# Splits on VectorE, gates one token group at a time, and candidate sums on GpSimd, in a two-block transformer kernel

## The chip, the cores and the metric

The kernel runs on one core of one Trainium2 chip. The core has five engines that run side by side, each with its own instruction queue in fixed order: TensorE (PE, matrix products; PEld is its weight load), VectorE (DVE), ScalarE (ACT), GpSimd (POOL) and SyncE (SP, which issues the transfers). The metric is the device time of one execution in microseconds (us), lower being better. The kernel before takes 1712.33 us, the median of three runs from 1710.88 to 1713.65.

## The reference

There are 256 tokens of 1024 features in fp32, and two blocks. The first adds to the tokens an attention and a recurrent mixer, and then a layer of experts that are looked up by keys; the part that the change touches is this layer:

```python
def peer_ffn(xn, wq, subkeys, u_tab, v_tab):
    q = (xt @ wq).reshape(T, PEER_HEADS, 2, PEER_HALF)
    s = jnp.einsum('thpd,hpnd->thpn', q, subkeys)
    top_s, top_i = lax.top_k(s, PEER_TOPK)
    cand_s = (top_s[:, :, 0, :, None] + top_s[:, :, 1, None, :]).reshape(...)
    best_s, best_j = lax.top_k(cand_s, PEER_TOPK)
    idx = jnp.take_along_axis(cand_i, best_j, axis=-1)
    gates = jax.nn.softmax(best_s, axis=-1)
    ...
    hdn = gelu(einsum('cd,chkd->chk', xc, u_tab[idx])) * gates
    out = einsum('chk,chkd->cd', hdn, v_tab[idx])
```

It has 8 heads, 2 halves of 128 keys, 16 best of each half, 16 best of their sums, and so 16 of 16,384 experts per head and token. The second block is a retention layer (`_retention_layer`), a layer norm, an attention with compressed keys (`_mla_layer`), and a layer norm; each is made of products of the tokens with large weights:

```python
    x = _layer_norm(DEEPNORM_ALPHA * x + y, ln_g[layer], ln_b[layer])
```

## The kernel before

**Products and splits.** Every weight comes from HBM in pieces of 128 by 1024 (`raw`). A product is made of three matmuls on rounded halves (`mm3`, whose matmuls are at line 344): ScalarE copies a piece to a rounded `whi`, and the rest `wlo` = `raw` − `whi` is one subtraction of 128x1024 on VectorE or GpSimd. This is called a split here. `split_next` issues a split when one of four places (`room`) is free, and chooses the engine of the subtraction by a letter: pieces of `peer_u` have "U" (GpSimd as long as `ex["pool_free"]` is true, else VectorE), those of `peer_v` "V" (VectorE), many others "A":

```python
            v, g = flow.clock["V"], flow.clock["G"]
            eng = "G" if g < v + state["slack"] else "V"
```

**The order of the work.** The program is written by generators. A planner (`Flow`) keeps an estimated clock for every engine; the main blocks run in a row (`flow.run`), and at each of their `yield`s the chains started by `flow.spawn` are looked at: a chain goes on when the planner's TensorE clock has passed the time that it yielded (`SOON` is an offset to that time), or when the condition it yielded holds. So the order of instructions on each engine is fixed when the program is written, by the planner's clocks and by where `yield` stands. Every engine's instruction goes through one helper, at line 264, so the profile names instructions by tiles.

**The experts.** All 16,384 experts are computed densely, in 64 steps of 256, and the gates choose: `up(i)` multiplies the tokens with a step of `peer_u` (48 products of 256 columns per half, into a bank `sm` of the accumulator memory), `weigh(i)` multiplies by the gate matrix, and `down(i)` multiplies with `peer_v` (24 products of 512 columns per half step, into `mm`). 22 `up` steps run before the first `down`, since the gates come late.

**The search.** Per head, `top_keys(h)` multiplies queries by keys, copies the scores to `s_`, and `best16` takes the 16 best of each of four rows on VectorE (`v` values, `w` values with those found struck out, `i` places). Then four additions make the candidate sums `cd`, and a second `best16` takes the 16 best of them (`bs`, `bj`). `ex["best"]` orders the heads. After heads 3 and 7 `decode(g)` turns the places into keys for four heads: it is about 80 small VectorE instructions, sets `pool_free` to false, and its end transposes the indices and gates (`GI`) on TensorE into `GT`.

**The gates.** `dense_gates` builds the gate matrix `gd` in four parts of 32 key rows each, the first (n = 0) before the first `down`, the others during the `up`/`down` turns. `gate_steps` takes groups of 8 tokens: VectorE writes `oq`, `oe` and two `op` per group, TensorE makes 16 (n = 0) or 8 (n > 0) matmuls into one `sm` bank, ScalarE copies, and for n > 0 VectorE adds the two halves (`gd<-sm,glo`), which frees the bank. The table `GATES` holds, for n = 0 and n > 0, the number of chains and the number of groups per step. At this time there are four `mm` and four `sm` banks, which `up` and the gates share.

**The second block.** Its layers run as products on TensorE with short chains between them: norms and rotations on VectorE (`rn_`, `l_r`, `lat`, `klat_`, `qlat_`, `ql`), and small products on GpSimd (`qr`, `ro`, `klfl`, `qlfl`). Before it, `state["slack"] = SLACK2` is set (line 1927), with the letter "A" for most pieces.

Of the kernel before, what the change touches and what calls it, by code (L numbers as in the profile page):

```python
# [287 lines left out]
NB = 32  # L288
LEAD = 16
AHEAD = 6  # L290
SOON = -600.0
NT = 8
CUT = 384
ADA0 = 3
SLACK = 2500.0
SLACK2 = 2000.0
NRAW = 4
NF = 8
BANKS = (3, 5)
# [4 lines left out]
NSP2 = 8  # L304
NL = 2
HOLD2 = 7
GATES = ((3, 1), (2, 2))
NGP = 4
HOLD3 = 8

# [2 lines left out]
def tile_blocks(ctx: ExitStack, tc: tile.TileContext, a, out):  # L313
# [3 lines left out]
    flow = Flow()  # L317
    V, G, S = Engine(nc.vector, flow, "V"), Engine(nc.gpsimd, flow, "G"), Engine(nc.scalar, flow, "S")
# [16 lines left out]
    def mm(o, l, r, first=True, last=True):  # L335
        n, m = r.free_size(), l.free_size()
        if l.dtype == F32:
            ns = max(4 * n / 2.36, 2 * m / 1.2)
        elif l.dtype == F32R:
            ns = n / 2.3 + 7.0  # L340
        else:
            ns = max(29.0, n / 2.4 + 2.5)
        flow.op("P", ns, o, (l, r))
        P.matmul(o, l, r, start=first, stop=last)  # L344

    def bank(tag="sm"):
        return psum["tiles"].tile([128, 512], F32, name=tag, tag=tag, bufs=psum[tag])
# [13 lines left out]
    def cst(name):  # L361
        k, s, e = TABS[name]
        return tabs[k][:, s:e]
# [17 lines left out]

        return (None, fn, src, None)

    ex = {"rest": 0, "sums": 0, "top": 0, "best": 0, "gates": 0, "built": 0, "used": 0, "pool_free": True}
    state = {"whole": 0, "dma": 0, "split": 0, "at": 0, "inuse": 1, "inuse2": 0, "slack": SLACK}
    raws, parts, came, freed, ring, nostart, spare = {}, {}, {}, [], {}, set(), set()
    whole, whole_freed = {}, []
# [114 lines left out]
    def piece(name, ch):  # L502
        pass_over()
        i = state["at"]
        assert order[i][0] == name and order[i][1] == ch, (order[i][:2], name, ch)
        state["at"] += 1
        if order[i][3] == "F":
            return raws.pop(i), i
        return parts.pop(i)
# [8 lines left out]
    def soon():  # L518

        pass_over()  # L520
        if order[state["at"]][3] == "F":
            more()
            yield flow.written[raws[state["at"]].name]
            return
        while state["at"] not in parts:
            more()
            if state["at"] not in parts:
                yield flow.written[raws[state["at"]].name]
        yield came[state["at"]]

    def mm3(o, wh, wl, xh, xl, first, last):
        mm(o, wh, xh, first, False)
        mm(o, wh, xl, False, False)
        mm(o, wl, xh, False, last)
# [365 lines left out]
    rest = order[before + 128:]  # L900
# [524 lines left out]
    gates = []  # L1425
# [136 lines left out]
    def wqt_turn(blk, tt, q):  # L1562
        yield 0
        if tt == 0:
            q2[blk] = [Bt.tile([128, 2, 256], F32, name="qf", tag="qf", bufs=4) for _ in range(2)]
        b = bank().rearrange("p (f t) -> p f t", f=4)
        for f in range(4):
            tr(b[:, f], q[:, f * 128:(f + 1) * 128])
        for h in range(2):
            S.activation(q2[blk][h][:, :, tt * 128:(tt + 1) * 128], b[:, 2 * h:2 * h + 2], AF.Copy)  # L1570
            if tt:
                flow.spawn(top_keys(2 * blk + h, q2[blk][h]))

    def wq_out(h, b):
        q = Bt.tile([128, 2, 256], F32, name="qf", tag="qf", bufs=4)
        S.activation(q, b, AF.Copy)
        flow.spawn(top_keys(h + 4, q))

    def best16(jobs, n):


        w = [Bt.tile([128, n], F32, name="w%d" % n, tag="w%d" % n, bufs=6) for _ in jobs]
        for v, ix, src in jobs:
            V.max(v[:, 0:8], src)
        yield SOON
        for (v, ix, src), t in zip(jobs, w):
            V.match_replace(t, v[:, 0:8], src, -3.0e38)
        for (v, ix, src), t in zip(jobs, w):
            V.max(v[:, 8:16], t)
        yield SOON  # L1590
        for v, ix, src in jobs:
            V.max_index(ix[:, 0:8], v[:, 0:8], src)
        yield SOON
        for (v, ix, src), t in zip(jobs, w):
            V.max_index(ix[:, 8:16], v[:, 8:16], t)

    def top_keys(h, q):
        yield lambda: ex["top"] == h and ex["best"] >= h - 1
        if h == 1:
            G.tensor_copy(io16, cst("iota16")[:, :, None].to_broadcast([128, 16, 64]))  # L1600
        b = bank()
        for tt in range(2):
            for p_ in range(2):
                o = (tt * 2 + p_) * 128
                mm(b[:, o:o + 128], q[:, p_, tt * 128:(tt + 1) * 128], sk[:, 2 * h + p_, :])
        s_ = Bt.tile([128, 4, 128], F32, name="s_", tag="s_", bufs=2)
        S.activation(s_, b4(b), AF.Copy)
        ex["top"] += 1
        yield 0
        yield lambda: ex["best"] == h  # L1610
        yield from best16([(v16[:, tt, 2 * h + p_, :], i16[:, tt, 2 * h + p_, :], s_[:, tt * 2 + p_, :])
                for tt in range(2) for p_ in range(2)], 128)
        yield SOON


        cd = Bt.tile([128, 2, 64], F32, name="cd", tag="cd", bufs=2)
        for i0, n, w, o in ((0, 1, 16, 0), (1, 3, 8, 16), (4, 4, 4, 40), (8, 8, 1, 56)):
            V.tensor_tensor(cd[:, :, o:o + n * w].rearrange("p t (i j) -> p t i j", i=n),
                            v16[:, :, 2 * h, i0:i0 + n, None].to_broadcast([128, 2, n, w]),
                            v16[:, :, 2 * h + 1, None, 0:w].to_broadcast([128, 2, n, w]), op=OP.add)  # L1620
        yield from best16([(bs[:, tt, h, :], bj[:, tt, h, :], cd[:, tt, :]) for tt in range(2)], 64)
        ex["best"] += 1
        if h % 4 == 3:
            flow.spawn(decode(h // 4))

    def decode(g):

# [8 lines left out]
        def t(name, dt=F32):  # L1636
            return Bt.tile([128, 2, 16, 4], dt, name=name, tag=name)
# [4 lines left out]
        V.tensor_scalar(i3, ip, 3, None, op0=OP.logical_shift_right)  # L1642
        yield SOON
        f1, f2, f3, fp = t("f1"), t("f2"), t("f3"), t("fp")
# [7 lines left out]
        V.tensor_scalar(m3, fp, 56.0, None, op0=OP.is_ge)  # L1652
        yield SOON
        row, cl = t("row", F16), t("cl", F16)
# [59 lines left out]
    def up(i):  # L1714
        b = bank().rearrange("p (e t) -> p e t", e=2)
        for e in range(2):
            yield from soon()
            hi, lo = piece("peer_u", i)
            for k in range(8):
                mm3(b[:, e, :], hi[:, k * 128:(k + 1) * 128], lo[:, k * 128:(k + 1) * 128], xn2[0][:, k, :], xn2[1][:, k, :],  # L1720
                    k == 0, k == 7)
                if k % 4 == 3 and (e, k) != (1, 7):
                    yield
        if LEAD < i < LEAD + AHEAD:
            yield lambda: "pool" in ex
            t = ex["ahead"][:, i - LEAD - 1]
        else:
            t = gh_tile()
        S.activation(t, b, AF.Gelu)
        GH[i] = t  # L1730
        yield

    def gh_tile():
        return B.tile([128, 2, 256], F32, name="gh", tag="gh", bufs=LEAD + 1)
# [139 lines left out]
    def dense_gates():  # L1874
# [5 lines left out]
        for n in range(128 // NB):  # L1880
            yield lambda: n == 0 or ex["used"] >= max(AHEAD, (n - 1) * NB // 2)
            g = Bg.tile([128, NB, 256], F32, name="gd", tag="gd", bufs=2)
            ex["shares"] = 0
            ways, at_once = GATES[n > 0]
            for j in range(ways):
# [6 lines left out]
    def experts():  # L1892
        for w, i in turns:
            yield from (up, down)[w](i)
# [31 lines left out]

    state["slack"] = SLACK2
    pc = tc.tile_pool(name="pc", bufs=1, reuse_waits="tile")
# [424 lines left out]
```

## Time and profile before

| what | value |
|---|---|
| median of three runs | 1712.33 us |
| profiled execution, its time | 1711.58 us |
| its span (first to last instruction) | 1709.8 us |
| TensorE busy | 1633.7 us, 96% |
| VectorE busy | 1205.4 us, 71% |
| ScalarE busy | 730.4 us, 43% |
| GpSimd busy | 427.1 us, 25% |

The profile is of one execution. Its time is 1.8 us more than its span. "Busy" counts the time in which an engine executes something; a busy TensorE isn't always at its peak, and its granted clock is told in the windows. A row of the chain of waits gives a start, a duration and what ran; a row of groups gives busy time, mean duration, the idle time in front and what ended it.

### The profile page before, as it was taken

To read this page: it belongs to the slowest core of one execution; us is meant where nothing else is said; L and a number is where in the kernel's file an instruction comes from. 1 tells how busy PE (TensorE), PEld (TensorE's weight loads), DVE (VectorE), ACT (ScalarE), POOL (GpSimd) and SP (SyncE) were. 2 spreads that over 40 slices of the span, in tenths; PEclk is the share of its full clock that TensorE was granted. 3 is DMA by queue.
4 is the path that set the end of the run, shared out by engine and by line. 5 is a ranking of instruction groups with operands and counts; after the bars stand their busy time and mean duration, and the time that the engine had idled before them with its cause. 6 is when DMAs were issued, how large, how long until landed. Compare 5 with 4: busy or idle time off the path is not lost.

```text
span 1709.8 us, 27783 instructions
## 1 busy us (share of the span) xinstructions
PE 1633.7 (96%) x10778; PEld 1407.3 (82%) x10778; DVE 1205.4 (71%) x2620; ACT 730.4 (43%) x1118; POOL 427.1 (25%) x226
## 2 busy tenths in 40 slices
PE   6999999999998999999999989999999998999997
PEld 5648798579997788898998879988797777998885
DVE  6598865479989799799858994476446446646655
ACT  1332321255454444445445445554543444554452
POOL 0042211161000000000000004410566884744343
PEclk9999999999998899999999999999999999999998
DMA  9562334454663455555665556666654563543342
GB/s 383 166 205 87 111 102 158 160 165 144 184 187 100 136 161 152 180 160 175 189 202 176 181 163 194 205 209 193 223 171 139 160 192 123 154 151 128 112 160 87
DMA packets 78616, 283.31 MB, mean 166 GB/s; under 512 B 9106, under 2 KB 9362, under 8 KB 77844
## 3 DMA queue, kind: packets, MB, share of 16 engines
q1 hardware_dynamic: 77188, 276.81, 51.5%
q10 hardware_dynamic: 1296, 4.72, 0.8%
q8 instruction: 84, 1.38, 0.3%
q14 instruction: 48, 0.39, 0.1%
HBM read 280.45 MB, written 1.05 MB: 165 GB/s over the span
## 4 chain that ended last, share of the span: by engine, by line
PE 72%; DVE 18%; issue 3%; POOL 3%; ACT 2%; DMA 1%; DVEq 0%; SPq 0%; ACTq 0%; POOLq 0%
PE mm L344 45%; PE sm L344 26%; DVE wlo L264 4%; DVE oq L264 2%; POOL wlo L264 2%; DVE op L264 2%; PE sm L369 1%; ACT whi L264 1%; DVE i L264 1%; DVE oe L264 1%; DVE v L264 1%; DVE gd L264 1%; DMA raw<-in_ada 1%; DVE x L264 1%; DVE w L264 1%
## 5 line engine op out<-in xcount | busy, mean ns | idle before, releaser
L264 ACT ACTIVATE whi<-raw 128x1024 fp32r<-128x1024 f32 (+1 forms) x415 | 430.6, 1043 | 257.8 <-PE mm L344 111.1
L264 DVE TENSOR_TENSOR wlo<-raw,whi 128x1024 fp32r<-128x1024 f32 (+1 forms) x284 | 377.6, 1339 | 172.7 <-ACT whi L264 171.7
L264 POOL TENSOR_TENSOR wlo<-raw,whi 128x1024 fp32r<-128x1024 f32 (+1 forms) x131 | 311.6, 2388 | 294.1 <-ACT whi L264 278.2
L344 PE MATMUL sm<-xh,whi 128*128 128x256 f32 x1024 | 293.4, 287 | 9.5 <-DVE gd L264 9.5
L344 PE MATMUL sm<-xh,wlo 128*128 128x256 f32 x1024 | 291.3, 285 | 1.6 <-DVE wlo L264 1.6
L344 PE MATMUL sm<-xl,whi 128*128 128x256 f32 x1024 | 290.8, 284 | 0.0
L344 PEld LDWEIGHTS sm<-xh,whi 128*128 128x128 f32 x1024 | 197.2, 193 | 13.6 <-DVE gd L264 12.4
L344 PE MATMUL mm<-whi,ah 128*128 128x512 f32 x512 | 204.5, 399 | 1.9 <-ACT ah L264 1.9
L344 PE MATMUL mm<-wlo,ah 128*128 128x512 f32 x512 | 201.0, 393 | 1.0 <-DVE wlo L264 1.0
L344 PEld LDWEIGHTS sm<-xh,wlo 128*128 128x128 f32 x1024 | 197.2, 193 | 2.5 <-DVE wlo L264 2.4
L344 PEld LDWEIGHTS sm<-xl,whi 128*128 128x128 f32 x1024 | 197.2, 193 | 1.2
L264 POOL TENSOR_TENSOR gt<-gt,raw 128x640 f32<-128x640 f32 (+2 forms) x16 | 33.6, 2099 | 585.0 <-ACT raw L264 551.1
L344 PE MATMUL mm<-whi,al 128*128 128x512 f32 x512 | 158.4, 390 | 0.0
L344 PEld LDWEIGHTS mm<-whi,al 128*128 128x128 f32 x512 | 96.4, 188 | 21.2
L344 PEld LDWEIGHTS mm<-whi,ah 128*128 128x128 f32 x512 | 96.9, 189 | 19.7 <-ACT ah L264 2.0
L344 PEld LDWEIGHTS mm<-wlo,ah 128*128 128x128 f32 x512 | 96.9, 189 | 19.6 <-DVE wlo L264 1.7
L344 PE MATMUL mm<-wlo,xh 128*128 128x512 f32 (+1 forms) x240 | 93.9, 391 | 5.9 <-POOL wlo L264 5.8
L344 PE MATMUL mm<-whi,xl 128*128 128x512 f32 (+1 forms) x240 | 93.3, 389 | 3.0 <-DVE xl L264 3.0
L344 PE MATMUL mm<-whi,xh 128*128 128x512 f32 (+1 forms) x240 | 95.8, 399 | 0.1
L264 DVE TENSOR_TENSOR al<-gh,ah 128x512 fp32r<-128x512 f32 x64 | 47.2, 737 | 68.2 <-ACT ah L264 68.2
L344 PE MATMUL mm<-xh,whi 128*128 128x256 f32 x328 | 94.8, 289 | 0.0
L344 PE MATMUL mm<-xh,wlo 128*128 128x256 f32 x328 | 92.8, 283 | 0.0
(544 smaller groups left out, 3134.6 us busy)
## 6 DMA issues: line engine op xcount, KB each, us to landing
raw<-in_peer_u SPq DMA_DIRECT2D x128, 512.0 KB, 3.8
raw<-in_peer_v SPq DMA_DIRECT2D x128, 512.0 KB, 4.5
raw<-in_ada SPq DMA_DIRECT2D x48, 512.0 KB, 5.0
raw<-in_wa_v SPq DMA_DIRECT2D x16, 512.0 KB, 4.8
raw<-in_wa_g SPq DMA_DIRECT2D x16, 512.0 KB, 4.5
raw<-in_wa_o SPq DMA_DIRECT2D x16, 512.0 KB, 4.3
raw<-in_wb_g SPq DMA_DIRECT2D x16, 512.0 KB, 4.3
raw<-in_wb_o SPq DMA_DIRECT2D x16, 512.0 KB, 3.8
```

Source lines behind the costliest of these rows:

```text
L264: return f(*args, **kw)
L344: P.matmul(o, l, r, start=first, stop=last)
L369: P.transpose(o, x, ident[0:x.shape[0], 0:x.shape[0]])
```

## The change

The diff has five parts. `SLACK2` becomes a large negative number, so every piece with the letter "A" in the second block is split on VectorE. `GATES` gives a step of one group, not two, for n > 0. The four additions for `cd` move from VectorE to GpSimd, with new conditions on `sums16` and `best`, so that the first search of the next head is written before the second search of this head; both `decode`s are spawned after head 7, so `pool_free` stays true longer. `SOON` goes from −600 to −1200. `up` yields after every k, not every fourth. No instruction is added or taken away on TensorE (11,111 both times); 385 splits instead of 284 are on VectorE, and 34 instead of 135 on GpSimd.

```diff
--- before.py
+++ after.py
@@ -288,12 +288,12 @@
 NB = 32
 LEAD = 16
 AHEAD = 6
-SOON = -600.0
+SOON = -1200.0
 NT = 8
 CUT = 384
 ADA0 = 3
 SLACK = 2500.0
-SLACK2 = 2000.0
+SLACK2 = -1e9
 NRAW = 4
 NF = 8
 BANKS = (3, 5)
@@ -304,7 +304,7 @@
 NSP2 = 8
 NL = 2
 HOLD2 = 7
-GATES = ((3, 1), (2, 2))
+GATES = ((3, 1), (2, 1))
 NGP = 4
 HOLD3 = 8
 
@@ -381,7 +381,7 @@
 
         return (None, fn, src, None)
 
-    ex = {"rest": 0, "sums": 0, "top": 0, "best": 0, "gates": 0, "built": 0, "used": 0, "pool_free": True}
+    ex = {"rest": 0, "sums": 0, "top": 0, "best": 0, "sums16": 0, "gates": 0, "built": 0, "used": 0, "pool_free": True}
     state = {"whole": 0, "dma": 0, "split": 0, "at": 0, "inuse": 1, "inuse2": 0, "slack": SLACK}
     raws, parts, came, freed, ring, nostart, spare = {}, {}, {}, [], {}, set(), set()
     whole, whole_freed = {}, []
@@ -1595,7 +1595,7 @@
             V.max_index(ix[:, 8:16], v[:, 8:16], t)
 
     def top_keys(h, q):
-        yield lambda: ex["top"] == h and ex["best"] >= h - 1
+        yield lambda: ex["top"] == h and ex["best"] >= h - 1 and ex["sums16"] >= h - 2
         if h == 1:
             G.tensor_copy(io16, cst("iota16")[:, :, None].to_broadcast([128, 16, 64]))
         b = bank()
@@ -1610,18 +1610,21 @@
         yield lambda: ex["best"] == h
         yield from best16([(v16[:, tt, 2 * h + p_, :], i16[:, tt, 2 * h + p_, :], s_[:, tt * 2 + p_, :])
                 for tt in range(2) for p_ in range(2)], 128)
-        yield SOON
+        ex["best"] += 1
 
 
         cd = Bt.tile([128, 2, 64], F32, name="cd", tag="cd", bufs=2)
         for i0, n, w, o in ((0, 1, 16, 0), (1, 3, 8, 16), (4, 4, 4, 40), (8, 8, 1, 56)):
-            V.tensor_tensor(cd[:, :, o:o + n * w].rearrange("p t (i j) -> p t i j", i=n),
+            G.tensor_tensor(cd[:, :, o:o + n * w].rearrange("p t (i j) -> p t i j", i=n),
                             v16[:, :, 2 * h, i0:i0 + n, None].to_broadcast([128, 2, n, w]),
                             v16[:, :, 2 * h + 1, None, 0:w].to_broadcast([128, 2, n, w]), op=OP.add)
+        yield 0
+        yield lambda: ex["sums16"] == h
         yield from best16([(bs[:, tt, h, :], bj[:, tt, h, :], cd[:, tt, :]) for tt in range(2)], 64)
-        ex["best"] += 1
-        if h % 4 == 3:
-            flow.spawn(decode(h // 4))
+        ex["sums16"] += 1
+        if h == 7:
+            for g in range(2):
+                flow.spawn(decode(g))
 
     def decode(g):
 
@@ -1719,7 +1722,7 @@
             for k in range(8):
                 mm3(b[:, e, :], hi[:, k * 128:(k + 1) * 128], lo[:, k * 128:(k + 1) * 128], xn2[0][:, k, :], xn2[1][:, k, :],
                     k == 0, k == 7)
-                if k % 4 == 3 and (e, k) != (1, 7):
+                if (e, k) != (1, 7):
                     yield
         if LEAD < i < LEAD + AHEAD:
             yield lambda: "pool" in ex
```

Three places of the instruction order, before and now. The first is GpSimd's order at the search, in the difference; `io_` is a constant, `cd` the sums of a head:

```order
 L264 TENSOR_TENSOR wlo<-raw,whi 128x1024 x10
 L264 CAST io_2556<-cona 128x1024
-L264 TENSOR_TENSOR wlo<-raw,whi 128x1024 x7
+L264 TENSOR_TENSOR cd<-v_2557 128x2x16
+L264 TENSOR_TENSOR cd<-v_2557 128x2x24
+L264 TENSOR_TENSOR cd<-v_2557 128x2x16
+L264 TENSOR_TENSOR cd<-v_2557 128x2x8
+L264 TENSOR_TENSOR wlo<-raw,whi 128x1024
+L264 TENSOR_TENSOR cd<-v_2557 128x2x16
```

GpSimd now has four `cd` additions of a head after a split or two of `peer_u`, eight times, where before were seven splits in a row. On VectorE the four `cd` are gone; the count of its splits from the first search to `irow`, the start of the gates, falls from 36 to 24, and from `irow` to the last group of part 0 it rises from 9 to 12. On TensorE 768 instead of 840 products of `up` stand ahead of the `GI` transposes, and 11 instead of 18 groups of part 0 are left behind the last of `up`'s products before the first `down`.

The second is VectorE's order in part 1 of the gates, before:

```order
L264 TENSOR_TENSOR wlo<-raw,whi 128x1024 x2
L264 TENSOR_TENSOR gh<-gh,gd 128x512
L264 TENSOR_TENSOR al<-gh,ah 128x512
L264 TENSOR_TENSOR gd<-sm,glo 128x32x8 x2
L264 TENSOR_TENSOR wlo<-raw,whi 128x1024
L264 TENSOR_TENSOR gd<-sm,glo 128x32x8 x2
L264 TENSOR_TENSOR wlo<-raw,whi 128x1024
L264 TENSOR_TENSOR oq<-irow,GT 128x1024
L264 TENSOR_TENSOR oe<-irow,GT 128x256
L264 TENSOR_TENSOR op<-oe,GT 128x256 x2
```

and now:

```order
L264 TENSOR_TENSOR wlo<-raw,whi 128x1024 x2
L264 TENSOR_TENSOR gd<-sm,glo 128x32x8
L264 TENSOR_TENSOR wlo<-raw,whi 128x1024
L264 TENSOR_TENSOR gd<-sm,glo 128x32x8
L264 TENSOR_TENSOR oq<-irow,GT 128x1024
L264 TENSOR_TENSOR oe<-irow,GT 128x256
L264 TENSOR_TENSOR op<-oe,GT 128x256 x2
L264 TENSOR_TENSOR wlo<-raw,whi 128x1024
L264 TENSOR_TENSOR oq<-irow,GT 128x1024
```

Before, a step adds the two groups in a pair of `gd` in a row behind two groups' `oq`, `oe`, `op`; now the `gd` come one by one with splits between. The number of gate matmul bursts on TensorE for n > 0 is about 96 instead of 48.

The third is GpSimd's order in the second block, in the difference:

```order
-L264 TENSOR_TENSOR wlo<-raw,whi 128x512 x2
-L264 TENSOR_TENSOR wlo<-raw,whi 128x1024 x5
-L264 TENSOR_TENSOR wlo<-raw,whi 128x512 x2
-L264 TENSOR_TENSOR wlo<-raw,whi 128x1024 x10
+L264 TENSOR_TENSOR qr<-ra,rb 128x256 x16
+L264 TENSOR_TENSOR ro<-ro,ga 128x512 x8
+L264 TENSOR_TENSOR klfl<-aff,klfh 128x256 x2
+L264 TENSOR_TENSOR qlfl<-aff,qlfh 128x256 x3
 L264 TENSOR_TENSOR h_72<-h_72,lnr 128x512 x2
```

Its 102 splits of the second block are gone, and what is left on GpSimd is the `qr`, `ro`, `klfl`, `qlfl` of the chains.

## Rows read from the trace of the kernel before

**Rows 1.** The page's engine line: busy us, share of the span, instructions.
```profile
PE 1633.7 (96%) x10778; PEld 1407.3 (82%) x10778; DVE 1205.4 (71%) x2620; ACT 730.4 (43%) x1118; POOL 427.1 (25%) x226
```

**Rows 2.** Table by stretches: busy us and instructions per engine, clock, DMA share.
```profile
368.00:504.00 136.00, 134.38 (x1106) 133.01 (x1105) 132.76 (x577) 68.30 (x82) 16.95 (x7) 1.00 0.53 160
...
597.00:703.00 106.00, 101.18 (x835) 87.91 (x833) 97.37 (x205) 49.42 (x79) 0.00 (x0) 1.00 0.52 158
...
1190.00:1710.00 520.00, 492.27 (x2868) 419.51 (x2866) 284.31 (x457) 230.17 (x354) 277.56 (x137) 0.98 0.48 151
```

**Rows 3.** Chain of waits, whole span: start us, us, what; the product pace.
```profile
603.72 2.83 PE mm L344 x12
...
609.88 5.75 PE sm L344 x48
...
709.28 5.47 PE mm L344 x24
```

**Rows 4.** Chain of waits in 366–384: the search of two heads on VectorE.
```profile
373.51 2.63 DVE cd L264 x4
...
377.95 0.76 DVE v L264 x4
...
382.62 0.55 DVE cd L264 x4
```

**Rows 5.** Groups in 368–425: busy us, mean ns, idle before; splits on both engines.
```profile
L264 POOL TENSOR_TENSOR wlo<-raw,whi 128x1024 fp32r<-128x1024 f32 x7 | 16.9, 2421 | 14.2 <-ACT whi L264 14.2
...
L264 DVE TENSOR_TENSOR wlo<-raw,whi 128x1024 fp32r<-128x1024 f32 x7 | 8.5, 1215 | 0.0
```

**Rows 6.** TensorE's timeline near 504 and 538: start us, us, instruction.
```profile
503.91 1.04 PE L369 MATMUL sm<-cona,GI 128*128 128x128 f32 x8
...
537.60 0.57 PE L344 MATMUL sm<-op,oq 128*128 128x32 f16 x16
```

**Rows 7.** Chain of waits in 500–612: VectorE between 516 and 520.
```profile
516.28 0.60 DVE oq L264
...
517.62 0.60 DVE oq L264
...
518.95 1.14 DVE wlo L264
```

**Rows 8.** TensorE's matmul groups in 538–562: busy us, mean ns, idle before, releaser.
```profile
L344 PE MATMUL sm<-op,oq 128*128 128x32 f16 x279 | 13.1, 187 | 10.1 <-DVE op L264 10.0
```

**Rows 9.** Table by stretches, TensorE alone: busy, granted clock, DMA share.
```profile
543.00:566.00 23.00, 13.71 (x231) 0.50 0.01 1
```

**Rows 10.** TensorE's waits in 597–1003: total us, times, longest.
```profile
PE sm L344 <- DVE gd L264: 9.5, 7, 4.4
```

**Rows 11.** TensorE's waits in the second block, 1190–1710.
```profile
PE mm L344 <- POOL wlo L264: 4.9, 6, 1.9
PE sm L369 <- DVE lat L264: 2.4, 1, 2.4
PE mm L344 <- DVE xl L264: 2.0, 1, 2.0
PE sm L369 <- DVE ql L264: 1.7, 1, 1.7
...
PE sm L369 <- DVE x L264: 1.2, 2, 0.8
```

**Rows 12.** Groups in 1190–1710: the splits of the second block.
```profile
L264 POOL TENSOR_TENSOR wlo<-raw,whi 128x1024 fp32r<-128x1024 f32 (+1 forms) x102 | 240.2, 2364 | 197.9 <-ACT whi L264 184.4 <-PE sm L369 8.4 <-PE sm L344 2.1
...
L264 DVE TENSOR_TENSOR wlo<-raw,whi 128x1024 fp32r<-128x1024 f32 (+1 forms) x42 | 74.6, 1777 | 101.8 <-ACT whi L264 101.8
```

**Rows 13.** Chain of waits in 1450–1470: VectorE's tiny instructions.
```profile
1458.66 0.17 DVE qlat_u L264
...
1463.52 2.33 DVE qlat_u L264
```

**Rows 14.** Groups by form on GpSimd: a small addition's nearest kin.
```profile
L264 POOL TENSOR_TENSOR rot<-qraw,sinn 128x128 f32<-128x128 f32 x4 | 2.1, 536 | 0.0
```

## The prediction

> **What bounds the kernel now.** First the page's busy shares: TensorE is busy 1633.7 us of a span of 1709.8, VectorE about seven tenths, GpSimd a quarter [rows 1]. So the question is where the other 76 us of TensorE lie, and where its busy time is not at full pace. Then the table by stretches [rows 2]: 368–504 has VectorE busy 132.76 of 136 us, so the search for the experts (top-16) runs as fast as VectorE lets it, with TensorE given product work beside it; in 597–703 VectorE is busy 97.37 of 106 (the gates of the later parts); in the second block, 1190–1710, only 284.31 of 520, while GpSimd is busy 277.56. Third the pace: 48 products of 256 columns took 5.75 us, 0.120 each, and 24 of 512 columns 5.47, 0.228 each [rows 3].
>
> Fourth the places where TensorE stands still. After its last `peer_u` product it has only the gate matmuls of part 0: they start alone at 537.60 [rows 6] and from 538 to 562 TensorE's waits there are for `op` from VectorE, 10.1 us in 279 matmuls [rows 8]; its clock in 543–566 is granted at 0.50, the 1.2 GHz level, after TensorE had stood idle between groups [rows 9]. VectorE's pace sets this stretch: the chain has one `oq` at 516.28 and the next at 517.62, so 1.34 us a group [rows 7], while the 16 matmuls of a group took 0.57 [rows 6]. Later, in 597–1003, TensorE waits 9.5 us in seven places for `gd`, the VectorE addition that frees a gate bank [rows 10]. In the second block it waits 4.9 us for `wlo` from GpSimd, and 2.4, 2.0 and 1.7 us for the VectorE results `lat`, `xl`, `ql` [rows 11].
>
> All sums are against the profiled execution, 1711.58 us, which is its span and 1.8 around it, and 0.75 below the median of 1712.33; I add that 0.75 at the end.
>
> **First part: the search and gate part 0.** Three edits act here: GpSimd forms the candidate sums `cd`; both decodes wait for head 7, which keeps `pool_free` true longer; and finer steps (`SOON`, a yield after every k). By the order, 9 of the `peer_u` splits go from VectorE to GpSimd net between the search's start and the last group of part 0 (12 fewer ahead of `irow`, 3 more behind), and VectorE loses 32 `cd` additions. A split costs VectorE 1.14 us in the chain [rows 7]. The sums of a head cost it 2.63 once and 0.55 next [rows 4]; eight heads at those two values make at most 2.63 + 7 × 0.55 = 6.5. The most that VectorE can be relieved by is 9 × 1.14 + 6.5 = 16.8 us.
>
> What of it reaches the end is less, because TensorE too needs something to do. Before the `GI` transposes, the last step of the decode (503.91, [rows 6]), stand 72 fewer products in the new order: 72 × 0.120 = 8.6 us earlier; 3 more splits stand behind it, 3 × 1.14 = 3.4, which leaves 5.2. A second count: the order leaves 11 instead of 18 groups of part 0 behind the last `peer_u` product; each of the 7 is worth 1.34 − 0.57 = 0.77 to TensorE, 5.4 in all. The bounds are 0 (the relief is eaten by another wait) and 16.8; I take 6, next to the two counts.
>
> GpSimd's cost: no row has an addition so small. Its nearest row is 128x128 at 0.536 us [rows 14], so four additions take between nothing and 2.1; I take 1. The sums of head h are needed after VectorE's first search of head h+1, which is 377.95 to 382.62, 4.67 us [rows 4]. One split ahead of them on GpSimd takes 2.42 [rows 5]: 3.4 together, hidden. With two splits it is 5.8, and VectorE would be late by 1.2 per head were it not for its own splits: 24 are left in 8 heads, 3.4 us a head. So I cost the additions at nothing; the search, with 1.81 for the second part (376.14 to 377.95, [rows 4]), and these splits give a period of 9.9 us. Without that cover it is 8 × 1.2 = 10.
>
> The adverse rule: the rows show `cd` at 2.63 us when a GpSimd split had just started and 0.55 without; but seven splits on VectorE in 368–425, among seven of GpSimd's, took 1.215 in the mean, and were not held [rows 5]. The Trainium skill (SBUF — State Buffer, "Who interferes with whom") says that a VectorE instruction with two SBUF inputs and a GpSimd instruction that reads SBUF exclude each other, the later one standing for the whole instruction. The `cd` row agrees, the splits' row does not show it; by the rule the first part would lose where more GpSimd work lies beside VectorE splits, and that is a rival below.
>
> **Second part: gate parts 1 to 3, one group per step.** Before, a step builds two groups, takes two of the four `sm` banks, and frees them only when both additions `gd` are through; now it takes one. VectorE's work is the same. What goes is at most the 9.5 us of `gd` waits. The longest, 4.4, ends behind a split that waited for its weights, and a bank less need not mend it: then 5.1. What comes: a switch of TensorE to the gate matmuls and back costs about 0.1 us (12 products after a burst took 2.83 instead of 12 × 0.228 = 2.73, [rows 3]), and the order has 48 more bursts: 4.8. So 9.5 − 4.8 = 4.7 at best, 5.1 − 4.8 = 0.3 in the middle, −4.8 at worst; I take 3.
>
> **Third part: the second block.** The 102 GpSimd splits (240.2 us, [rows 12]) go to VectorE: 102 × 1.14 = 116 us, which makes 400 of 520 if nothing comes back. But something does: VectorE's tiny instructions stand still under a GpSimd split, `qlat_u` 0.17 free and 2.33 beside one [rows 13]. So a split is ready 1.2 us sooner (1.14 for a mean of 2.36), and the 4.9 us waits for GpSimd's `wlo` go; the chains of tiny operations behind `lat`, `xl`, `ql` shorten, and with them up to 6.1 us of waits. At most 11.0. Against it: a split queued on VectorE ahead of a chain holds it for 1.14; three chains, 3.4. That leaves 7.6; I take 8. The chain `qr`, `ro`, `klfl`, `qlfl`, which stays on GpSimd, now finds it empty. The lower bound is the slower rival.
>
> Sum: 6 + 3 + 8 = 17; 1711.6 − 17 + 0.7 = 1695.
>
> **Rivals.**
> *The second block gives nothing*: VectorE's queue puts splits ahead of the small chains as often as GpSimd blocked them before. For it: VectorE splits already waited 101.8 us for `whi`, 2.42 for each of the 42 [rows 12], and what is queued behind waits too. Against: it has 120 us to spare. Time: 1711.6 − 9 + 0.7 = 1703.
>
> *GpSimd holds VectorE in the search* (the rule above): 9 more GpSimd splits, each holding a VectorE instruction for up to 2.42: 21.8 against the 16.8 relieved, so gate part 0 starts 5.0 later: 1711.6 + 5.0 − 11 + 0.7 = 1706. For it the 2.63; against it the seven undisturbed splits.
>
> *More than I count*: the full 16.8 in the first part and the full 11.0 in the third, 3 in the second: 1712.3 − 30.8 = 1681.
>
> *Nothing net*: the three parts cancel, or the planner's new order only moves the waits. 1712.
>
> *Slower*: in the second block TensorE waits in five places for what VectorE's small chains give (`lat`, `xl`, `ql` and twice `x`, 1.2 us) [rows 11]. With 144 instead of 42 splits on VectorE, each such result stands behind a split that itself waits for its `whi` at the head of the queue: 1.14 + 2.42 = 3.56. Five times 3.56 is 17.8, against 9 us from parts one and two: 1712.3 + 8.8 = 1721. It is slower from four of the five on. For it: VectorE's order is fixed when the program is written. Against it: a VectorE that is late finds `whi` ready, so that wait shrinks when the queue fills.
>
> **Chances.** 0.56 for 1695 (own range 1687 to 1703), 0.14 for 1703, 0.06 for 1706, 0.08 for 1681, 0.07 for no change, 0.09 for slower. What a measurement of this kernel can tell from no change is about 0.2%, 3.4 us: faster 0.84, the same 0.07, slower 0.09. The range 1681 to 1708 leaves out no change, slower and a little below.
>
> **What the changed profile would show.** First part: the search stretch still full on VectorE, the `GI` transposes about 5 us earlier beside TensorE's products of the same work, some 15 instead of 25 us of gate matmuls alone, with the 0.50 clock stretch shorter by as much; `bs` on VectorE never waiting for GpSimd's `cd`. Second: the `gd` wait of TensorE near 4 instead of 9.5. Third: GpSimd nearly idle from 1190 on, `qlat_u` at 0.17 throughout, no TensorE wait for GpSimd `wlo`, and TensorE's idle time in the block smaller by 8 us; VectorE busy under 400. I am wrong if TensorE waits for VectorE `wlo` in the second block by more than 5 us, if `bs` waits for `cd`, or if the gate bursts cost more than 0.1 us each.

## The result

The changed kernel takes 1686.1 us, the median of four runs from 1684.65 to 1687.64, against 1711.92 before (the median of four, where the forecast had three): the ratio is 0.985 with a 95% interval of 0.983 to 0.987. The forecast was 1695 with a range of 1681 to 1708. The profiled execution took 1684.77 us, with a span of 1683.0; that span is 26.8 us shorter than the one of before.

The first row after is the page's engine line, to be held against [rows 1]:

```profile
PE 1628.0 (97%) x10778; PEld 1405.6 (84%) x10778; DVE 1238.0 (74%) x2689; ACT 738.1 (44%) x1118; POOL 206.4 (12%) x157
```

TensorE's busy time fell by 6 us, the span by 27: most of what went are waits. VectorE has only 33 us more, though it took over more than a hundred splits of 1.14 us. GpSimd's time halved.

The table of the stretches follows; its rows answer to those of [rows 2], and the bounds follow the work; the middle one is 7 us longer than its row before (bounds from the span's start, length, busy time of PE, PEld, DVE, ACT, POOL with instructions, granted clock, DMA share, GB/s).

```profile
368.00:493.00 125.00, 125.00 (x1037) 124.31 (x1035) 116.19 (x532) 65.03 (x78) 44.53 (x48) 1.00 0.54 164
...
590.00:703.00 113.00, 113.00 (x897) 101.31 (x897) 100.88 (x198) 57.64 (x84) 0.00 (x0) 1.00 0.55 171
1188.50:1683.00 494.50, 476.37 (x2816) 409.47 (x2815) 316.26 (x555) 224.32 (x346) 40.16 (x32) 0.99 0.50 155
```

In the search TensorE is busy for the whole 125 us, and VectorE, which was at its limit before, is busy 116 of them. In the stretch of the later gates TensorE had 101.18 of 106 before and is busy for all of its 113 now (106.00 of 106 in 589–695). In the second block VectorE went from 284 in 520 us to 316 in 494.5, and GpSimd from 278 to 40.

By four marks in each trace (the start of the first search on VectorE, the first and the last product with `peer_v`, the last matmul) the gain divides so, in us, with the experiments of below beside it:

| kernel | search to first `peer_v` | `peer_v` part | second block |
|---|---|---|---|
| before | 194.1 | 638.8 | 495.2 |
| changed | 186.2 | 633.8 | 481.4 |
| only SLACK2 | 194.1 | 638.8 | 481.4 |
| SLACK2 and GATES | 194.2 | 635.6 | 481.4 |
| SLACK2 and finer steps | 190.9 | 635.2 | 481.4 |
| changed, old GATES | 186.1 | 635.7 | 481.4 |
| changed, old search | 190.9 | 633.4 | 481.4 |
| changed, coarse steps | 187.8 | 636.3 | 481.4 |
| changed, early decode | 184.7 | 635.2 | 481.4 |
| changed, all `peer_u` splits on VectorE | 191.4 | 633.5 | 481.4 |
| changed, `peer_u` splits on GpSimd longer | 215.9 | 635.2 | 481.4 |

So 7.9, 5.0 and 13.8 us came from the three parts, where the forecast had 6, 3 and 8. Each mark comes from one trace, and the start of the search differs by up to 2 us between traces of kernels that are alike up to there; within the parts a difference under about 1 us says nothing. The experiments ran in three groups, in which the kernel before had medians of 1712.4 to 1713.4 us, beside the 1711.92 here; so 1.5 us between times of two groups says nothing either; there the ratios and the parts decide.

GpSimd's groups in the search, 368–455, show what the candidate sums cost there (busy us, mean ns, idle before and its releasers):

```profile
L264 POOL TENSOR_TENSOR wlo<-raw,whi 128x1024 fp32r<-128x1024 f32 x16 | 38.3, 2404 | 8.6 <-ACT whi L264 6.3 <-DVE i L264 2.3
L264 POOL TENSOR_TENSOR cd<-v 128x32 f32<-128x32 f32 (+2 forms) x32 | 6.8, 245 | 6.9 <-DVE v L264 6.9
```

The sums take 0.245 us each in the mean, 0.98 a head; VectorE waits for `cd` once, 2.3 us. The gate matmuls alone on TensorE, in 538.6–554.8 (compare [rows 8]), and the clock behind them (compare [rows 9]):

```profile
L344 PE MATMUL sm<-op,oq 128*128 128x32 f16 x176 | 7.8, 186 | 6.4 <-DVE op L264 6.4
```

```profile
543.00:557.00 14.00, 8.13 (x133) 0.50 0.02 8
```

There are 176 of them (11 groups) instead of 288, in 16 us instead of 25; TensorE still waits for `op`, and its clock is granted at 0.50 in 543–557, against 543–566 before. Then TensorE's waits of the gates, 590–1003, all that are left where [rows 10] had 9.5 us:

```profile
PE mm L344 <- ACT ah L264: 3.4, 1, 3.4
```

Its waits in the second block (compare [rows 11]):

```profile
PE mm L344 <- DVE xl L264: 2.1, 1, 2.1
PE sm L369 <- POOL ro L264: 1.3, 1, 1.3
PE mm L344 <- DVE wlo L264: 1.2, 2, 0.8
PE sm L344 <- POOL qr L264: 0.5, 1, 0.5
PE sm L369 <- DVE x L264: 0.4, 1, 0.4
```

Here 4.9, 2.4 and 1.7 us (GpSimd's `wlo`, `lat`, `ql`) are gone; `xl` stays at 2.1, and `ro` and VectorE's `wlo` cost 1.3 and 1.2. VectorE's groups of the block:

```profile
L264 DVE TENSOR_TENSOR wlo<-raw,whi 128x1024 fp32r<-128x1024 f32 (+1 forms) x141 | 167.7, 1198 | 101.5 <-ACT whi L264 100.6
...
L264 DVE SCALAR_TENSOR_TENSOR rn_r<-rn_u,rn_r 128x1 f32<-128x1 f32 x24 | 4.7, 196 | 0.8
```

A split takes 1198 ns in the mean, where the 42 of before took 1777 [rows 12]. The row of before that answers to the second one is:

```profile
L264 DVE SCALAR_TENSOR_TENSOR rn_r<-rn_u,rn_r 128x1 f32<-128x1 f32 x24 | 19.3, 804 | 0.8
```

Twenty-four tiny instructions on 128 numbers fell from 804 to 196 ns in the mean. The chain of `qlat_u`, of which [rows 13] showed 2.33 us a step, in VectorE's timeline (start, us, instruction, idle time before):

```profile
1432.48 1.23 DVE L264 TENSOR_TENSOR wlo<-raw,whi 128x1024 fp32r<-128x1024 f32 x1 [0.58 <-ACT whi L264]
1433.62 0.15 DVE L264 TENSOR_TENSOR qlat_u<-qlat_r 128x2 f32<-128x2 f32 x1
1433.81 0.16 DVE L264 TENSOR_TENSOR qlat_u<-qlat_u,qlat_x 128x2 f32<-128x2 f32 x1
1434.01 0.16 DVE L264 SCALAR_TENSOR_TENSOR qlat_r<-qlat_u,qlat_r 128x2 f32<-128x2 f32 x1
...
1436.05 1.23 DVE L264 TENSOR_TENSOR wlo<-raw,whi 128x1024 fp32r<-128x1024 f32 x1
1437.20 0.15 DVE L264 TENSOR_TENSOR qlat_u<-qlat_r 128x2 f32<-128x2 f32 x1
```

Each step takes 0.16 us. Something else is new here: splits stand between the steps of the chain, 3.6 us from one `qlat_u` group to the next. The queue that the slower rival spoke of is there, but TensorE has no wait for `ql` any more.

### The profile page after: what moved, and what is told of

The parts are those of the page before. It is cut to its first block, busy times and chain, and to the rows that moved or that the text cites. A ratio compares the mean times of both kernels' runs of the same rounds, so it can differ in the third digit from the quotient of the medians.

```text
span 1683.0 us, 27724 instructions
## 1 busy us (share of the span) xinstructions
PE 1628.0 (97%) x10778; PEld 1405.6 (84%) x10778; DVE 1238.0 (74%) x2689; ACT 738.1 (44%) x1118; POOL 206.4 (12%) x157
## 4 chain that ended last, share of the span: by engine, by line
PE 88%; DVE 8%; ACT 2%; issue 1%; DMA 1%; POOL 0%; ACTq 0%; DVEq 0%; SPq 0%; POOLq 0%
PE mm L344 53%; PE sm L344 33%; PE sm L369 1%; DVE wlo L264 1%; ACT whi L264 1%; DVE op L264 1%; DVE oq L264 0%; DVE h L264 0%; DVE x L264 0%; DVE ny L264 0%; DVE acc L264 0%; DVE n_r L264 0%; DMA xs<-in_x 0%; DVE ma L264 0%; DMA raw<-in_ada 0%
## 5 line engine op out<-in xcount | busy, mean ns | idle before, releaser
L264 DVE TENSOR_TENSOR wlo<-raw,whi 128x1024 fp32r<-128x1024 f32 (+1 forms) x381 | 469.3, 1237 | 172.0 <-ACT whi L264 170.4
L264 POOL TENSOR_TENSOR wlo<-raw,whi 128x1024 fp32r<-128x1024 f32 x34 | 82.8, 2444 | 122.4 <-ACT whi L264 118.9
L344 PE MATMUL mm<-xl,whi 128*128 128x256 f32 x328 | 92.8, 283 | 0.0
```

The costliest lines, as they stand in the source:

```text
L264: return f(*args, **kw)
```

## The experiments

**SLACK2 alone.** From the kernel before:

```diff
-SLACK2 = 2000.0
+SLACK2 = -1e9
```

> The kernel before with SLACK2 alone changed: all 102 GpSimd splits of the second block go to VectorE. Theory (the parts add; in the trace the block from the last expert product to the last matmul fell from 495.2 to 481.4 us): 13.7 us faster, 1698, ratio 0.992. Rival (the block gains only because the search and the gates arrive differently): 1712, ratio 1.000.

Measured: 1697.9 us, ratio 0.991 (0.990 to 0.993). The second block took 481.4 us, as in the changed kernel, and the two other parts did not move; the `gd` waits are as before:

```profile
PE sm L344 <- DVE gd L264: 9.4, 7, 4.4
```

So the splits' part stands by itself, and is the largest of the three: more than half of the gain.

**The gates back.** From the changed kernel:

```diff
-GATES = ((3, 1), (2, 1))
+GATES = ((3, 1), (2, 2))
```

> The changed kernel with GATES back to two groups per step. Theory (one group per step is what takes away the TensorE waits for gd, 9.5 us before and none after, less the cost of more bursts): 5 us slower than the changed kernel, 1691, ratio to before 0.988, and gd waits of 8 to 10 us come back in the trace. Rival (the finer yields of up took them away): 1686, ratio 0.985, no gd wait.

Measured: 1686.8 us, ratio 0.984 (0.983 to 0.986), not to be told from the changed kernel. All of TensorE's waits in 590–1003 are:

```profile
PE mm L344 <- ACT ah L264: 6.0, 1, 6.0
PE sm L344 <- DVE wlo L264: 1.5, 1, 1.5
PE mm L344 <- DVE wlo L264: 1.0, 1, 1.0
```

No wait for `gd` came back. The theory fell, and the rival had the time and the wait right: in this change the group size is not what takes them away. The time of the `peer_v` part rose by 1.9 us in the trace, below what the runs can tell.

**SLACK2 and GATES.** From the kernel before, both lines of the two diffs above as the change has them.

> The kernel before with SLACK2 and GATES changed, nothing else. Theory G (one group per step by itself takes the TensorE waits for gd away, the finer steps or the new search would have done so too): no gd wait of TensorE in 597-1003, and 4 to 6 us less than with SLACK2 alone (1697.9): 1692 to 1694. Rival F (the finer steps took them away, GATES does nothing): gd waits of 9 us stay, 1698.

Measured: 1695.9 us, ratio 0.990 (0.989 to 0.992), 2.0 below SLACK2 alone, half of the least that the theory had. The waits in 590–1003:

```profile
PE sm L344 <- DVE op L264: 3.7, 2, 2.6
PE mm L344 <- ACT ah L264: 2.3, 1, 2.3
```

The `gd` wait is gone, so the group size does take it away where nothing else does; but 3.7 us of waits for `op` stand in its place. The `peer_v` part is 3.1 us shorter than with SLACK2 alone: the 9.4 us of waits were exchanged for others and for more bursts. The bursts were cheap: TensorE has 94 of them instead of 48, and its busy time in the part rose from 628.7 to 630.0 us.

**SLACK2 and the finer steps.** From the kernel before, with SLACK2 as above and:

```diff
-SOON = -600.0
+SOON = -1200.0
-                if k % 4 == 3 and (e, k) != (1, 7):
+                if (e, k) != (1, 7):
```

> The kernel before with SLACK2 and the finer steps (SOON, yields of up), nothing else. Theory G: the finer steps alone also change the gd waits, 1692 to 1695, and with 14 instead of 18 groups of part 0 left 3 us of it come from there. Rival (only GATES does it): gd waits of 9 us stay, 1695 to 1698.

Measured: 1692.4 us, ratio 0.988 (0.986 to 0.990), 5.5 below SLACK2 alone: 3.2 in the search, 3.6 in the `peer_v` part. The waits:

```profile
PE mm L344 <- ACT ah L264: 6.0, 1, 6.0
PE sm L344 <- DVE wlo L264: 1.5, 1, 1.5
PE mm L344 <- DVE wlo L264: 1.0, 1, 1.0
```

The finer steps do it as well, and they also shorten the search. So the two edits do the same work twice: each takes away the `gd` waits, for 3 to 4 us in the part, and both together give 5. The rival that the finer steps do nothing there fell as well.

**The finer steps back.** From the changed kernel, the reverse of the last diff.

> The changed kernel with SOON at -600 and up yielding every fourth k. Theory (finer steps only shift the order a little: 14 instead of 11 groups of part 0 are left behind the last up product, 3 x 0.77 us): 2 us slower, 1688, ratio 0.986. Rival (the finer steps carry the first part's gain): 1692 or more, ratio 0.989.

Measured: 1689.5 us, ratio 0.986 (0.985 to 0.988). Its runs (1688.5 to 1689.7) lie above all of the changed kernel's, though the intervals of the two ratios overlap. 1.6 us are in the search, 2.5 in the `peer_v` part: theory and rival had all of it ahead of the first `peer_v` product, and the time is between them.

**The old search.** From the changed kernel, the whole of `top_keys` as before; of the difference these lines:

```diff
-            G.tensor_tensor(cd[:, :, o:o + n * w].rearrange("p t (i j) -> p t i j", i=n),
+            V.tensor_tensor(cd[:, :, o:o + n * w].rearrange("p t (i j) -> p t i j", i=n),
...
-        yield lambda: ex["sums16"] == h
...
-        if h == 7:
-            for g in range(2):
-                flow.spawn(decode(g))
+        if h % 4 == 3:
+            flow.spawn(decode(h // 4))
```

> The changed kernel with the old top_keys: candidate sums on VectorE, decode after heads 3 and 7. Theory (VectorE's load in the search sets when gate part 0 ends: 12 more splits and the sums come back to it): gate part 0 ends 6 to 8 us later, 1692 to 1694, ratio 0.989. Rival (the finer steps did the most of it): 1688 or less, ratio 0.986.

Measured: 1690.6 us, ratio 0.987 (0.986 to 0.989), 4.5 above the changed kernel; the first `peer_v` product is 4.7 us later. That is less than the 6 to 8 expected, the rest of the 7.9 being the finer steps'.

**The early decode.** From the changed kernel, only the last five lines of that diff.

> The changed kernel with decode of heads 0 to 3 spawned after head 3 again; the sums stay on GpSimd. The order has 32 instead of 24 VectorE splits in the search. Theory (the time of gate part 0 follows VectorE's splits): 7 x 1.14 = 8 us more on VectorE, of which 4 to 8 reach the end: 1690 to 1694. Rival (the sums on GpSimd carry the gain): 1686 to 1688.

Measured: 1685.6 us, ratio 0.984 (0.983 to 0.986): no slower than the changed kernel, with eight more splits on VectorE ahead of `irow` (32 instead of 24) and one fewer behind it. The theory fell. When the decodes start does not matter here, and these seven splits do not carry the gain. By the difference to the old search, what carries it is the sums on GpSimd together with the next head's search ahead of the second one; no run has one of these two without the other.

**All `peer_u` splits on VectorE.** From the changed kernel:

```diff
-            eng = "G" if ex["pool_free"] else "V"
+            eng = "V"
```

> The changed kernel with every peer_u split on VectorE, also in the search: GpSimd has only the candidate sums there. Theory (VectorE is not at its limit in the changed search; a GpSimd split holds it about as long as it saves): 1685 to 1690. Rival (each split on VectorE costs its 1.14 us at the end of gate part 0): 15 to 18 more, some 16 us later, 1698 to 1702.

Measured: 1691.2 us, ratio 0.987 (0.986 to 0.989). It is 5 us slower, all of it in the search (191.4 instead of 186.2): VectorE has 15 more splits ahead of `irow` (39 instead of 24) and four fewer between `irow` and the first `peer_v` product. These 11 cost 5.2 us of the 13 that they take. The theory named too little and the rival too much.

**The splits on GpSimd longer.** From the changed kernel:

```diff
-        ex["pool_free"] = False
...
             ex["built"] = n + 1
+            ex["pool_free"] = False
```

> The changed kernel with the splits of peer_u staying on GpSimd through the decode and gate part 0: 33 more splits leave VectorE. Theory (GpSimd's splits hold VectorE's two-input instructions in the decode and the gates, up to 2.36 us each): oq, oe, op and the decode grow, gate part 0 ends later by 0 to 15 us, 1687 to 1700. Rival (VectorE is only relieved, 33 x 1.14 = 38 us, and TensorE's 11.8 us of idle gate time go): 1675.

Measured: 1715.9 us, ratio 1.002 (1.001 to 1.003), 30 above the changed kernel. VectorE was not relieved; the `GI` transposes, the end of the decode, came 29 us later. VectorE's groups of the decode's additions in 455–522, and then, in 368–455, two groups of one view: the search's places and the decode's first additions; in this kernel:

```profile
L264 DVE TENSOR_TENSOR eq<-eq 128x256 f16<-128x256 f16 (+2 forms) x23 | 24.0, 1041 | 0.8
```

```profile
L264 DVE FIND_INDEX8 i<-v,w 128x8 uint32<-128x128 f32 x32 | 8.5, 285 | 0.0
...
L264 DVE TENSOR_TENSOR eq<-eq 128x512 f16<-128x512 f16 (+1 forms) x2 | 5.0, 2475 | 0.1
```

and in the changed kernel, where GpSimd is idle in the decode and has 16 splits in the search:

```profile
L264 DVE TENSOR_TENSOR eq<-eq 128x512 f16<-128x512 f16 (+2 forms) x12 | 3.7, 312 | 0.3
```

```profile
L264 DVE FIND_INDEX8 i<-v,w 128x8 uint32<-128x128 f32 x32 | 8.5, 285 | 0.0
```

The fp16 additions of two inputs grew from 312 to 1041 ns in the mean, the first two, one of 128x512 and one of 128x256, to 2475. FIND_INDEX8 took 285 ns in both, but both have GpSimd splits under the search. The kernel before has none after 397; its row of 400–470, with GpSimd idle:

```profile
L264 DVE FIND_INDEX8 i<-v,w 128x8 uint32<-128x128 f32 x16 | 4.3, 286 | 0.0
```

So a GpSimd split holds VectorE in the decode, and not in the search. That is why keeping GpSimd off the decode is worth its splits, and why 16 splits under the search are cheap.

**Reading on GpSimd in the second block.** From the changed kernel, in `split_next`:

```diff
+        if state["slack"] < 0:
+            G.eng.tensor_tensor(r, r, hi[:, :n].bitcast(F32), op=OP.add)
         came[i] = flow.written[r.name]
```

> The changed kernel, with one addition on GpSimd of the size of a split behind each VectorE split of the second block: it reads raw and whi and writes raw, which nobody uses after that; the result is not changed. Theory (before, GpSimd's reading held VectorE's two-input instructions: qlat_u 2.33 instead of 0.17): the tiny chains are held again, and 6 to 10 of the 13.7 us of the second block come back: 1693 to 1697. Rival (the gain came from the shorter split itself, 1.14 instead of 2.36 us): 1686 to 1688.

Measured: 1822.5 us, ratio 1.064 (1.063 to 1.066). The groups of the second block:

```profile
L471 POOL TENSOR_TENSOR raw<-raw,whi 128x1024 f32<-128x1024 f32 (+1 forms) x140 | 384.9, 2769 | 171.1 <-DVE wlo L264 158.5 <-DVE qlat_u L264 6.6 <-DVE klat_u L264 2.5
L264 DVE TENSOR_TENSOR wlo<-raw,whi 128x1024 fp32r<-128x1024 f32 (+1 forms) x141 | 277.9, 1990 | 53.6 <-ACT whi L264 53.3
...
L264 DVE SCALAR_TENSOR_TENSOR rn_r<-rn_u,rn_r 128x1 f32<-128x1 f32 x24 | 14.4, 600 | 0.8
```

VectorE's split rose from 1198 to 1990 ns, the tiny `rn_r` from 196 to 600. The theory has the sign, but the time is 136 us longer instead of 6 to 10. This edit does more than put the reading back: GpSimd now has an addition for every piece, where before it had 102 splits; each piece's transfer buffer is freed only when the addition is done; and the small GpSimd products queue behind. So it shows the hold, and not what the hold was worth in the kernel before.

**Writing only.** The same place, with memsets:

```diff
+        if state["slack"] < 0:
+            for m in (n, n, n * 5 // 8):
+                G.eng.memset(r[:, :m], 0.0)
```

> As the run with the additions, but GpSimd writes raw with memsets of about the same time and reads nothing; the result is not changed. Theory (only GpSimd's reading holds VectorE): 1686 to 1688, and qlat_u at 0.17. Rival (any GpSimd work on this memory does, or the later freeing of raw): as the run with the additions, 1693 to 1697.

Measured: 1715.2 us, ratio 1.002 (1.001 to 1.003). The groups, and TensorE's two longest waits:

```profile
L472 POOL MEMSET raw<- 128x1024 f32 (+3 forms) x432 | 348.1, 818 | 122.6 <-DVE wlo L264 106.0
L264 DVE TENSOR_TENSOR wlo<-raw,whi 128x1024 fp32r<-128x1024 f32 (+1 forms) x141 | 167.8, 1196 | 112.8 <-ACT whi L264 111.3 <-PE sm L369 0.6
...
L264 DVE SCALAR_TENSOR_TENSOR rn_r<-rn_u,rn_r 128x1 f32<-128x1 f32 x24 | 6.6, 274 | 0.8
```

```profile
PE sm L369 <- POOL ro L264: 13.2, 7, 4.5
PE sm L344 <- POOL qr L264: 5.9, 2, 5.4
```

GpSimd was busy with them for 348 us of the block, and VectorE's split took 1196 ns: what it takes with GpSimd idle. The four longest `rn_r`, 333 to 1282 ns, each ran beside a GpSimd product `ro`, which reads. So for VectorE's instructions of two inputs not GpSimd's activity but its reading counts. That is not so for all of VectorE's instructions: one in the chain that has a single input, 170 ns in the changed kernel, took 575 here, until the first of two memsets beside it had ended (VectorE's and GpSimd's timelines):

```profile
1461.98 0.57 DVE L264 TENSOR_SCALAR qlat_x<-qlat_ss 128x2 f32<-128x2 f32 x1 [0.34 <-ACT qlfh L264]
```

```profile
1461.42 1.80 POOL L472 MEMSET raw<- 128x1024 f32 x2
```

The 29 us that the kernel lost are of another kind: some 17 of them are in these waits for `ro` and `qr` (1.8 in the changed kernel), products that now share GpSimd's queue with the memsets, and 12 in TensorE's busy time in the block (488.0 instead of 476.4 us, with the clock granted at 0.97 in the mean instead of 0.99). The expected time was wrong for that reason; the expected durations were right but for such instructions. Both runs hold each piece back and load GpSimd's queue (348 us here, 385 with the additions), and with the additions VectorE's splits took 110 us longer: by this comparison most of the 107 us between the two runs goes with the reading, which is an estimate.

**The first block on VectorE.** From the changed kernel:

```diff
-SLACK = 2500.0
+SLACK = -1e9
```

> The changed kernel with the first block's splits of free choice on VectorE too (SLACK as SLACK2): four of GpSimd's go to VectorE. Theory (as in the second block, GpSimd's reading holds VectorE): 1 to 4 us faster, 1682 to 1685. Rival (four splits are too few, and not on the path): 1686.

Measured: 1690.8 us, ratio 0.987 (0.985 to 0.989), 5 us slower. Six splits moved by the trace, four ahead of the search and two at the start of the second block. In the trace 2.6 us are lost ahead of the search, where TensorE has a new wait of 2.3 us for `n2y`, and 2.6 in the second block, where its waits for `xl` (3.8 us instead of 2.1) and VectorE's `wlo` (2.2 instead of 1.2) are longer. Neither theory named that; why the new order makes these waits was not tested. None of these kernels beats the changed one beyond the noise.

## Why the prediction was right

The time fell as forecast, and each of the three parts gained; the sum of 17 was 9 us short. At 1686.1 the time lies inside the stated range but just below the forecast's own 1687 to 1703, towards the rival "more than I count": the second and the third part each gave more than the most that the prediction allowed them.

**The second block (8 forecast, 13.8 measured; 11.0 was the bound).** The mechanism was right: the splits alone give it, and the tiny chains run free now; that GpSimd's reading had held them is what the runs with additions and memsets show. The term was mis-sized. I took 3.4 us off for chains queued behind splits; that queue is there, but all TensorE's listed waits of the block are 5.5 us now. Before they were 14.8, with short ones that I left out of the bound, these two among them:

```profile
PE mm L344 <- ACT ogh L264: 1.2, 1, 1.2
...
PE sm L344 <- DVE rp L264: 0.9, 1, 0.9
```

So 9.3 of the 13.8 are waits. The rest is in TensorE's busy time, which the bound did not count; between the marks, before and now (start and end, length, busy, clock):

```profile
1202.03:1697.19 495.16, 480.23 (x2814) 0.99 0.49 153
```

```profile
1188.96:1670.38 481.42, 475.91 (x2814) 1.00 0.51 157
```

It fell by 4.3 us for the same matmuls, with the granted clock a little higher. How much of the 9.3 comes from sooner splits (4.9 of them were waits for GpSimd's `wlo`) and how much from the freed chains (4.1 for `lat` and `ql`) no run separates. The estimate of VectorE's load, 400 us at the most, was far above the 316. Its busy time from the first mark of the block on, before, was 277.71:

```profile
1201.60:1710.00 508.40, 480.67 (x2816) 410.59 (x2814) 277.71 (x451) 224.11 (x346) 275.17 (x136) 0.98 0.48 151
```

The 101 splits at 1.14 would have added 115 to it, so by this estimate some 76 us of the 277.7 had been standing under GpSimd.

**The search (6 forecast, 7.9 measured).** Near, in part by luck. The sums moved at almost no cost, as I had it (0.98 us a head, with one wait of 2.3), but not under the cover that I named: VectorE's first split in the stretch starts at 425.57, after the last search, so a head took about 6.7 us and not 9.9. And I counted in splits relieved, 9 at 1.14, and the runs refute that currency: seven more splits on VectorE cost nothing, eleven cost 5.2. I took the finer steps as part of the relief, and they gave 1.6 to 3.2 by themselves.

**The gates (3 forecast, 5.0 measured; 4.7 was the bound).** The step that failed is that one group per step takes away the `gd` waits. It can, alone, and gains 3.1 us in the part, about the 3 forecast, with new waits for `op`; but the finer steps, which I costed at nothing there, take them away as well, and with them the group size is worth no more than the runs can tell. The 4.4 us wait, which I thought might stay, went by either edit. The bursts were costed too high, 4.8 us for 48: with one group per step TensorE's busy time in the part is 1.3 us longer without the finer steps (628.7 to 630.0) and 2.9 with them (627.4 to 630.4), which is 0.03 to 0.06 a burst.

**The rivals.** The lock in the search, 21.8 us for nine more GpSimd splits, didn't come: the search's instructions are not held by GpSimd, as the 285 ns with splits beside them and the 286 without show, and the sums, of which one had stood for a split, are no longer on VectorE. My argument against it was a misreading, though. The seven VectorE splits that I called undisturbed [rows 5] did not run beside GpSimd's seven, but after them (minimum, median and maximum in ns, first and last start):

```profile
L264 POOL TENSOR_TENSOR wlo<-raw,whi x7: 2380/2397/2578, 373.4 to 393.7; 128x1024 fp32r<-128x1024 f32 x7
L264 DVE TENSOR_TENSOR wlo<-raw,whi x7: 1205/1218/1220, 402.1 to 423.2; 128x1024 fp32r<-128x1024 f32 x7
```

So they said nothing about the lock, and the decode with GpSimd's splits beside it shows it at work. The Trainium skill (SBUF — State Buffer, "Who interferes with whom") says that a VectorE instruction with two SBUF inputs contends with a GpSimd instruction that reads SBUF and not with one that only writes it; the split (1990 beside reads, 1196 beside memsets) and the decode's additions (1041 and 312) agree with it. The slower rival, chains behind waiting splits, is seen in the timeline and had no price.

**The signs named.** GpSimd nearly idle in the second block, `qlat_u` at 0.16, no TensorE wait for GpSimd's `wlo` there, VectorE under 400, and the shorter stretch at the 0.50 clock all came. TensorE's listed waits in the block fell by 9.3 us, not 8. The `GI` transposes came 11.6 us earlier, not 5, which is more than the 72 fewer products ahead of them (8.6) alone; the `gd` waits went to nothing, not to 4; VectorE was a little less full in the search, 116.19 of 125 us. Of the three signs of being wrong one came: `bs` waited for `cd`, once, 2.3 us. TensorE's waits for VectorE's `wlo` (1.2 us) and the price of a burst stayed below their marks.

## What to carry to other kernels

Before work is shared out between VectorE and GpSimd by their loads, look at what the tiny VectorE instructions take beside a GpSimd read: here 102 reading splits on GpSimd cost VectorE, by the estimate above, some 76 us of standing still, and giving VectorE all of them left it at 64% in the block and TensorE with little more than a third of its waits. Where GpSimd does help is under instructions that it does not hold, here the key search. When several edits of a change aim at one wait, take them out one by one: here the edit named for the gates was hardly needed once the finer steps were in.

## What the runs showed of the hardware

What GpSimd's work costs VectorE depends on what both do with the memory. 348 us of memsets left a VectorE split at 1196 ns, and additions that read made it 1990; yet a TENSOR_SCALAR on 128x2 went from 170 to 575 ns beside a memset. I had not expected that the search's instructions (FIND_INDEX8, 285 ns) pay nothing at all beside 2.4 us splits, when a 128x512 addition of the decode, 418 ns in the changed kernel, took up to 2.5 us beside one. Nor that small additions on GpSimd are so short: 0.245 us in the mean over 128x16, 128x32 and 128x48, less than half of the nearest row of before, which is 128x128.
